# Three instead of two seven-product pairs per gate-up group of an encoder layer, with the weight sums formed by adding transfers

## The chip, the cores and the metric

The kernel runs on one core of one Trainium2 chip. Its time is the device time of one execution in microseconds (us). The engines are TensorE (PE, with its weight loads, PEld), VectorE (DVE), ScalarE (ACT), GpSimd (POOL) and SyncE (SP), which here issues transfers only.

## The reference

One layer of an encoder works on x of 256 x 2048 in float32: two gated feed-forward blocks with a mixer between them (an input projection, a bidirectional gated recurrence in eight heads, windowed attention in eight heads, an output projection). The change touches the two feed-forward blocks:

```python
D_MODEL, SEQ, D_FF = 2048, 256, 5632
def swiglu(x, w_gate_up, w_down):
    gate, up = jnp.split(x @ w_gate_up, 2, axis=-1)
    return (jax.nn.silu(gate) * up) @ w_down
ff = swiglu(rms_norm(x, pre_norm_ffn1), w_ffn1_gate_up, w_ffn1_down)
x = x + 0.5 * rms_norm(ff, post_norm_ffn1)
...                                     # the mixer
ff = swiglu(rms_norm(x, pre_norm_ffn2), w_ffn2_gate_up, w_ffn2_down)
x = x + 0.5 * rms_norm(ff, post_norm_ffn2)
```

Gate-up multiplies 256 x 2048 by 2048 x 11264, down 256 x 5632 by 5632 x 2048.

## The kernel before

**Matmuls in three products.** A float32 operand is split into two parts of a shorter format: ACT casts it to its high part (`h`), DVE subtracts that from the source to get the low part (`l`; `split_act`, lines 175 to 177). A product is then h·h + h·l + l·h, three matmuls of 128x512 outputs (`three`, line 417). All weights are split like this as they come in: SP issues the load of a pair's weights, 2 x 128 rows by 1024 columns, into a `raw` tile of 128x2048 (three of these), and each half of it, 128x1024, is cast by ACT and subtracted by DVE into `h` and `l` tiles (five each). PE reads these.

**Pairs, plain and of seven products.** A pair `u` of row blocks meets two column blocks and two halves (m) of the 256 tokens: a 2x2 by 2x2 block product. Plain, that takes eight block products, 24 matmuls. `seven` (line 445) does it as a Strassen-like scheme with seven, 21 matmuls. It needs sums of the weight blocks b11, b12, b21, b22 and of the activations' blocks. The weights' sums are made by DVE in the raw tile: line 455 writes b11+b12 and b12+b22 over the first two blocks (one instruction of 128x1024), line 459 adds to b22, line 461 to b21 (128x512 each); splits of b11, of the lower half, the upper half and the lower half again lie between. Four of the products go into PSUM banks of their own (`p`), three straight into the running sums `c`. `fold` (line 489) adds the p banks to c behind the last seven of a group.

**Gate-up** (`Gated`, line 793) goes over 11 groups `g` of 512 gate and 512 up columns, each over eight pairs of rows. In groups 1 to 10 the pairs 2 and 4 (`MIXED_IN`) are sevens; group 0 is plain in all pairs, as the sums of activations for these pairs are prepared in it (`even`, line 860, behind `spread`; the result is an `xs` tile per pair). Behind each group `units` (line 881) multiplies silu(gate) by up into `z` and `s`, and behind the first pair of the next group PE transposes them into two banks, four transposes each; ACT and DVE split the result into `ht`, the activations of down. For those pairs of down that are sevens (`MIXED`, 11 of 22), ACT first copies the bank to `z` (line 905) and DVE forms the sums of activations (`sums_of`, line 378) into a tile that stays.

**Down** (`Pairs`, line 540) goes over its 22 pairs twice, once for each half of the 2048 columns, in the order of a hand-written list per run. 11 pairs in each run are sevens. Their activations' sums are split anew in each run into an `sp` tile (`left_sums`, line 569), except for pairs 0 and 2, which the second run takes over.

**What sets the order.** Each engine runs its instructions in the order of the program; semaphores hold an instruction until its operands are there and its target is free. PSUM has eight banks, four each for the names `pa` and `pb`: four for c, four for p or transposes, handed on in turn. Loads are issued by SP as raw tiles come free.

Of the kernel before, what the change touches and what calls it, by code (L numbers as in the profile page):

```python
# [37 lines left out]
def hymba_layer_kernel(  # L38
# [347 lines left out]

    class Blocks:
# [4 lines left out]
        AHEAD = False  # L392
        ahead = None
# [43 lines left out]

        def one_block(self):

            return (  # L440
                p.tile([P, 1024], F32R, tag=t, name=nm(t))[:, 0:512]
                for p, t in ((hip, "h"), (lop, "l"))
            )

        def seven(self, u, aside=None):

            raw = load(self.source(u))
            if aside:
# [6 lines left out]
            nc.vector.tensor_tensor(  # L455
                four[:, 0:2], four[:, 0::3], four[:, 1:2].to_broadcast([P, 2, 512]), ALU.add
            )
            lower = split_half(raw, 1)
            nc.vector.tensor_tensor(b22, b11, b22, ALU.add)  # L459
            upper = split_half(raw, 0)  # L460
# [79 lines left out]
    class Pairs(Blocks):  # L540
# [7 lines left out]
        def __init__(self, w, orders, tiles, sums, room, gain_src, keep=()):  # L548

            super().__init__(tiles, sums)  # L550
            self.keep, self.kept = keep, {}
# [17 lines left out]
        def left_sums(self, u):  # L569
            if u in self.kept:  # L570
                return self.kept[u]
            keep = self.now == 0 and u in self.keep
            tag = f"sp{u}" if keep else "sp"
            w = far["pool"].tile([P, 4, 2, P], F32R, tag=tag, name=nm("sp"), bufs=1 if keep else 2)
            split_act(w[:, :, 0, :], w[:, :, 1, :], self.sums[u])
            if keep:
                self.kept[u] = w
            return w

# [11 lines left out]
        def folded(self):  # L591
            if self.now == 0:
                wide = self.room.tile([P, 2, 512], F32, tag="sp", name=nm("y"), bufs=2)
                y = [
                    [
                        self.room.tile([P, 512], F32, tag="z", name=nm("y")),
                        self.room.tile([P, 512], F32, tag="s", name=nm("y")),
                    ],
                    [wide[:, i, :] for i in range(2)],
                ]  # L600
            else:
# [185 lines left out]
    MIXED_IN = (2, 4)  # L787
# [5 lines left out]
    class Gated(Blocks):  # L793
# [11 lines left out]
        def source(self, u):  # L805
            return self.w[:, 2 * u : 2 * u + 2, :, self.g * 512 : (self.g + 1) * 512]

# [29 lines left out]
    def ffn(gated, w_dn, post_gain, again, gain=None, lead=None, aside=None):  # L837

        with ExitStack() as st:
# [5 lines left out]
            where_X_was = []  # L845

            def room_for(tag):
                return work.tile([P, 512], F32, tag=tag, name=nm(tag))

            def sums_room(u):  # L850
                n = MIXED.index(u)
                if n == 0:
# [677 lines left out]
```

## Time and profile before

Three executions took 1866.74, 1863.61 and 1865.3 us, median 1865.3. The profile was taken of a further execution, of which it gives the span, from the first instruction to the last:

| | us |
|---|---|
| median of three executions | 1865.3 |
| profiled execution: span | 1861.4 |
| what the median has beyond that span | 3.9 |
| PE busy | 1840.7 |
| DVE busy | 1576.6 |
| ACT busy | 1086.1 |
| POOL busy | 21.4 |

"Busy" is the time in which an engine has an instruction under way; a PE that is busy without a gap is not therefore at its peak. The groups name line, engine, operation, target and source tiles, shapes and count, then total and mean duration and the idle time ahead of them with what released it. A stretch is a piece of the span with the busy time of each engine in it, the granted clock of PE, the mean busy share of the 16 DMA engines and what they moved.

### The profile page before, as it was taken

How to read it: one execution, taken by the hardware profiler on the slowest of the kernel's cores; microseconds unless marked ns; L12 is line 12 of the kernel's file. 1: busy time of each engine (PE TensorE's matmuls, PEld its weight loads, DVE VectorE, ACT ScalarE, POOL GpSimd, SP SyncE). 2: the span in 40 equal slices, each digit the busy share in tenths (PEclk: the TensorE clock that was granted, in tenths of full speed). 3: DMA queues.
4: the chain of work that ended last, by engine and by line, in shares of the span. 5: the costliest groups of instructions: out<-in, count | busy, mean ns of one | idle time of the engine just before them, and what ended most of it. 6: DMA issues, size and time to landing. Idle time of an engine off the chain costs nothing.

```text
span 1861.4 us, 23279 instructions
## 1 busy us (share of the span) xinstructions
PE 1840.7 (99%) x8658; PEld 1527.0 (82%) x8658; DVE 1576.6 (85%) x1988; ACT 1086.1 (58%) x1445; POOL 21.4 (1%) x39
## 2 busy tenths in 40 slices
PE   9999999999999999999999999999999999999997
PEld 6888888888878777888888887788888888878886
DVE  7978888888899998567787788888888788899997
ACT  6555555555566565676677655655555555566563
POOL 1000000000000000000000000000000000000000
PEclk9999999999999999999999999999999999999999
DMA  7555655555555465655565455565565556445564
GB/s 251 204 200 187 208 196 181 181 203 203 188 204 215 179 255 196 201 181 166 169 187 148 169 210 200 185 214 186 211 207 192 199 195 207 175 181 205 224 228 168
DMA packets 180880, 365.78 MB, mean 197 GB/s; under 512 B 9256, under 2 KB 56448, under 8 KB 180000
## 3 DMA queue, kind: packets, MB, share of 16 engines
q1 hardware_dynamic: 180416, 364.17, 56.2%
q8 instruction: 68, 1.11, 0.2%
q14 instruction: 44, 0.36, 0.1%
q0 software_dynamic: 352, 0.14, 0.0%
HBM read 360.06 MB, written 4.21 MB: 196 GB/s over the span
## 4 chain that ended last, share of the span: by engine, by line
PE 72%; DVE 17%; DMA 4%; ACT 3%; issue 3%; POOL 0%; SPq 0%; DVEq 0%; ACTq 0%; POOLq 0%
PE pa L423 28%; PE pb L423 26%; DVE l L177 9%; PE pa L299 8%; PE pa L304 4%; DMA raw<-in_w_ffn_down_dram 2%; DVE raw L455 2%; ACT h L176 2%; DVE raw L459 1%; DVE raw L461 1%; DVE la L177 1%; DMA raw<-in_w_ffn_gate_up_dram 1%; PE pa L354 1%; PE pa L352 1%; PE pa L353 1%
## 5 line engine op out<-in xcount | busy, mean ns | idle before, releaser
L176 ACT CAST h<-raw 128x1024 fp32r<-128x1024 f32 (+1 forms) x793 | 795.0, 1028 | 616.2 <-PE pb L423 316.7
L177 DVE TENSOR_TENSOR l<-raw,h 128x1024 fp32r<-128x1024 f32 (+1 forms) x793 | 925.9, 1192 | 202.3 <-ACT h L176 168.8
L423 PE MATMUL pa<-h,xt 128*128 128x512 f32 x1248 | 431.3, 392 | 0.0
L423 PE MATMUL pb<-h,xt 128*128 128x512 f32 x1168 | 407.3, 390 | 0.0
L423 PEld LDWEIGHTS pa<-h,xt 128*128 128x128 f32 x1248 | 234.1, 188 | 48.7 <-ACT h L176 0.8
L423 PEld LDWEIGHTS pb<-h,xt 128*128 128x128 f32 x1168 | 219.2, 188 | 46.0 <-DVE xt L232 0.5
L423 PE MATMUL pa<-l,xt 128*128 128x512 f32 x624 | 243.3, 390 | 0.1
L423 PE MATMUL pb<-l,xt 128*128 128x512 f32 x584 | 227.3, 389 | 0.0
L299 PE MATMUL pa<-xt,h 128*128 128x512 f32 x672 | 164.7, 394 | 0.0
L423 PE MATMUL pa<-h,ht 128*128 128x512 f32 x440 | 156.1, 390 | 0.4 <-ACT h L176 0.4
L423 PE MATMUL pb<-h,ht 128*128 128x512 f32 x440 | 155.0, 390 | 0.2
L299 PEld LDWEIGHTS pa<-xt,h 128*128 128x128 f32 x672 | 123.0, 188 | 23.6
L423 PEld LDWEIGHTS pa<-l,xt 128*128 128x128 f32 x624 | 117.2, 188 | 24.5 <-DVE l L177 1.1
L423 PEld LDWEIGHTS pb<-l,xt 128*128 128x128 f32 x584 | 109.7, 188 | 22.6
L455 DVE TENSOR_TENSOR raw<-raw 128x1024 f32<-128x1024 f32 x88 | 107.5, 1222 | 1.6
L423 PEld LDWEIGHTS pa<-h,ht 128*128 128x128 f32 x440 | 82.4, 188 | 18.7 <-ACT h L176 1.3
L423 PEld LDWEIGHTS pb<-h,ht 128*128 128x128 f32 x440 | 82.6, 188 | 17.9 <-DVE pb L501 1.0
L304 PE MATMUL pa<-xt,l 128*128 128x256 f32 x672 | 91.5, 285 | 0.0
L304 PEld LDWEIGHTS pa<-xt,l 128*128 128x128 f32 x672 | 87.1, 191 | 3.2
L423 PE MATMUL pa<-l,ht 128*128 128x512 f32 x220 | 86.2, 392 | 1.5 <-DVE l L177 1.5
L423 PE MATMUL pb<-l,ht 128*128 128x512 f32 x220 | 86.0, 391 | 0.1
L423 PE MATMUL pb<-h,sp 128*128 128x512 f32 x192 | 70.1, 395 | 2.3 <-ACT h L176 2.3
(281 smaller groups left out, 2179.4 us busy)
## 6 DMA issues: line engine op xcount, KB each, us to landing
raw<-in_w_ffn_gate_up_dram SPq DMA_DIRECT2D x350, 512.0 KB, 4.6
raw<-in_w_ffn_down_dram SPq DMA_DIRECT2D x88, 1024.0 KB, 5.4
raw<-in_w_mix_in_dram SPq DMA_DIRECT2D x52, 1024.0 KB, 5.0
raw<-in_w_mix_out_dram SPq DMA_DIRECT2D x16, 1024.0 KB, 5.0
pg<-in_post_norm_ffn_dram SPq DMA_DIRECT2D x4, 512.0 KB, 6.9
X<-in_x_dram SPq DMA_DIRECT2D x2, 1024.0 KB, 7.4
bias<-row SPq DMA_DIRECT2D x16, 128.0 KB, 4.6
kept<-X SPq DMA_DIRECT2D x2, 1024.0 KB, 4.9
```

The lines of the kernel that those rows point to most:

```text
L176: nc.scalar.copy(hi, src)
L177: nc.vector.tensor_tensor(lo, src, hi.bitcast(F32), ALU.subtract)
L299: nc.tensor.matmul(slot[f], weights(hs, kk, f), xcol(xt, k), start=(k == 0), stop=(k == KT - 1))
L304: nc.tensor.matmul(slot[f][:, 0:T], weights(ls, kk, f), xcol(xt, kh * 8 + kk, 0), start=False, stop=False,)
L352: nc.tensor.matmul(dst, xh, h[:, o : o + n], start=(k == 0), stop=False)
L353: nc.tensor.matmul(dst, xh, l[:, o : o + n], start=False, stop=False)
L354: nc.tensor.matmul(dst, xl, h[:, o : o + n], start=False, stop=(k == KT - 1))
L423: nc.tensor.matmul(self.bank(at), lhs, rhs, start=(n == 1), stop=n in (ends, self.of[at]), skip_group_check=n > ends,)
L455: nc.vector.tensor_tensor(four[:, 0:2], four[:, 0::3], four[:, 1:2].to_broadcast([P, 2, 512]), ALU.add)
L459: nc.vector.tensor_tensor(b22, b11, b22, ALU.add)
L461: nc.vector.tensor_tensor(b21, b22, b21, ALU.add)
```

## The change

- `MIXED_IN` becomes (1, 3, 5): three sevens per group in groups 1 to 10. With pair 5 as the last seven, the fold goes to the beginning of pair 7 (before: of pair 6).
- A class `Summed` keeps two slots of 128x1024 in the room in which x was. A slot gets b11 and b12 by a transfer on POOL's queue, then b12 and b22 by an adding transfer on top, and holds then what line 455 made. When a seven has split its upper half the slot is free, and is filled for the seven after the next one of the list. SP loads only b11 and, together, b21 and b22 for such a seven.
- All 30 sevens of a gate-up do that, and in down every second one in the order of a run (6 of 11); the other sevens of down, and those of the output projection, keep the instruction on DVE.
- The sums of activations for down are split once, when they are made, in a third slot of that room, and stored to DRAM by POOL; down loads them (`left_early`, on SP, ahead of the weights of that seven). `z` and `s` live in the fourth slot.
- `units` does all eight transposes before the copies and splits.

```diff
+    class Summed:
...
+        def fill(self, slot):
+            if self.n == len(self.jobs):
+                return
+            key, (k0, n1) = self.jobs[self.n]
+            self.n += 1
+            two = slot.rearrange("p (i c) -> p i c", i=2)
+            nc.gpsimd.dma_start(two, k0)
+            nc.gpsimd.dma_start(two, n1, accum_op=ALU.add)
+            self.filled[key] = slot
+
+        def take(self, key):
+            return self.filled.get(key)
+
+        def free(self, key):
+            self.fill(self.filled.pop(key))
...
         def seven(self, u, aside=None):
 
-            raw = load(self.source(u))
+            two = self.summed.take(self.key(u)) if self.summed else None
+            self.left_early(u)
+            if two is None:
+                raw = load(self.source(u))
+            else:
+                raw = rawp.tile([P, 2048], F32, tag="raw", name=nm("raw"))
+                src = self.blocks(u)
+                nc.sync.dma_start(raw[:, 0:512], src[:, 0, 0])
+                nc.sync.dma_start(
+                    raw[:, 1024:2048].rearrange("p (i c) -> p i c", i=2), src[:, 1]
+                )
...
-            nc.vector.tensor_tensor(
-                four[:, 0:2], four[:, 0::3], four[:, 1:2].to_broadcast([P, 2, 512]), ALU.add
-            )
+            if two is None:
+                nc.vector.tensor_tensor(
+                    four[:, 0:2], four[:, 0::3], four[:, 1:2].to_broadcast([P, 2, 512]), ALU.add
+                )
+                two = raw
             lower = split_half(raw, 1)
-            nc.vector.tensor_tensor(b22, b11, b22, ALU.add)
-            upper = split_half(raw, 0)
+            nc.vector.tensor_tensor(b22, two[:, 0:512], b22, ALU.add)
+            upper = split_half(two, 0)
+            if two is not raw:
+                self.summed.free(self.key(u))
             nc.vector.tensor_tensor(b21, b22, b21, ALU.add)
...
         def left_sums(self, u):
-            if u in self.kept:
-                return self.kept[u]
...
+            if u in self.left:
+                return self.left.pop(u)
+            w = far["pool"].tile(
+                [P, 4, 2, P], F32R, tag="sp", name=nm("sp"), bufs=4 if self.stored else 2
+            )
+            if self.stored:
+                nc.sync.dma_start(w.bitcast(F32), self.sums[u])
+            else:
+                split_act(w[:, :, 0, :], w[:, :, 1, :], self.sums[u])
             return w
...
-    MIXED_IN = (2, 4)
+    MIXED_IN = (1, 3, 5)
...
-                for j in range(2):
-                    bank = (pa, pb)[j]()
+                banks = [pa(), pb()]
+                for j, bank in enumerate(banks):
                     for i in range(2):
...
+                for bank in banks:
                     g = len(hts)
...
-                        sums[g] = sums_of(u, sums_room(g))
+                        ws = sums_of(u, room_for("s").rearrange("p (j t) -> p j t", j=4))
+                        w = where_X_was(2).rearrange("p (j i t) -> p j i t", j=4, i=2)
+                        split_act(w[:, :, 0, :].bitcast(F32R), w[:, :, 1, :].bitcast(F32R), ws)
+                        sums[g] = dram.tile([P, 4, 2, P], F32, tag=f"ss{g}", name=nm("ss"))
+                        nc.gpsimd.dma_start(sums[g], w)
...
+                        if u == 6:
+                            gated.summed = Summed(
...
+            rows.summed = Summed(
+                gated.summed.slots,
+                [
+                    ((now, u), (b[:, 0], b[:, :, 1]))
+                    for now in range(2)
+                    for u in [u for u in orders[now] if u in sums][::2]
+                    for b in [rows.blocks(u, now)]
+                ],
+            )
+            rows.summed.begin()
```

Three places show what moves. First PE behind a group boundary of the first feed-forward block, from the last transpose on; `pa` and `pb` are PSUM banks, `xt` the activations, `xs` their sums. Before, the next pair is plain:

```order
L898 MATMUL pb_435_2395<-ident_79,s_422_2340 128x128
L423 MATMUL pa_423_2343<-h_438_2406,xt_11_123 128x512
L423 MATMUL pa_423_2343<-l_439_2407,xt_11_123 128x512
L423 MATMUL pa_423_2343<-h_438_2406,xt_11_123 128x512
L423 MATMUL pa_424_2344<-h_438_2406,xt_11_123 128x512
L423 MATMUL pa_424_2344<-l_439_2407,xt_11_123 128x512
L423 MATMUL pa_424_2344<-h_438_2406,xt_11_123 128x512
L423 MATMUL pb_425_2345<-h_438_2406,xt_11_123 128x512
```

The same place now:

```order
L955 MATMUL pb_558_3142<-ident_79,rooms_71_475 128x128 x4
L450 MATMUL pa_571_3188<-h_563_3168,xt_11_123 128x512
L450 MATMUL pa_571_3188<-l_564_3169,xt_11_123 128x512
L450 MATMUL pa_571_3188<-h_563_3168,xt_11_123 128x512
...
L450 MATMUL pb_574_3191<-h_567_3177,xs_72_480 128x512
L450 MATMUL pb_574_3191<-l_568_3178,xs_72_480 128x512
L450 MATMUL pb_574_3191<-h_567_3177,xs_72_480 128x512
L450 MATMUL pb_573_3190<-h_569_3184,xs_72_480 128x512
L450 MATMUL pb_573_3190<-l_570_3185,xs_72_480 128x512
L450 MATMUL pb_573_3190<-h_569_3184,xs_72_480 128x512
```

Where a plain pair went on in the c banks, a seven takes new banks at once: pa_571 first, and pb_573, the sixth of its seven block products (p2), is the bank that pb_558, the second transposes, had. The written-out order holds 7270 matmuls of 128x512, 60 fewer than before.

Second, DVE from the end of `units`' product to the splits of the transposed banks (`ht`) and the sums of activations. Before:

```order
L177 TENSOR_TENSOR l_574_3126<-raw_572_3122,h_573_3125 128x512
L455 TENSOR_TENSOR raw_572_3122<-raw_572_3122 128x1024
L177 TENSOR_TENSOR l_576_3131<-raw_572_3122,h_575_3130 128x1024
L459 TENSOR_TENSOR raw_572_3122<-raw_572_3122 128x512
L461 TENSOR_TENSOR raw_572_3122<-raw_572_3122 128x512
L177 TENSOR_TENSOR l_578_3136<-raw_572_3122,h_577_3135 128x1024
L177 TENSOR_TENSOR ht_564_3073<-z_563_3071,ht_564_3073 128x2x256
L380 TENSOR_TENSOR sums_109_681<-z_563_3071 128x256
L177 TENSOR_TENSOR ht_566_3084<-pb_565_3079,ht_566_3084 128x2x256
```

And now:

```order
L177 TENSOR_TENSOR l_566_3173<-raw_562_3165,h_565_3172 128x1024
L177 TENSOR_TENSOR l_568_3178<-rooms_71_475,h_567_3177 128x1024
L501 TENSOR_TENSOR raw_562_3165<-rooms_71_475,raw_562_3165 128x512
L505 TENSOR_TENSOR raw_562_3165<-raw_562_3165 128x512
L177 TENSOR_TENSOR l_570_3185<-raw_562_3165,h_569_3184 128x1024
L177 TENSOR_TENSOR l_577_3217<-raw_575_3213,h_576_3216 128x1024
L177 TENSOR_TENSOR ht_559_3152<-rooms_71_475,ht_559_3152 128x2x256
L380 TENSOR_TENSOR rooms_71_475<-rooms_71_475 128x256
L177 TENSOR_TENSOR ht_561_3162<-pb_558_3142,ht_561_3162 128x2x256
```

The double sum is gone (the slot in `rooms` holds it), and behind the seven's last split one split of the following pair (l_577) now stands ahead of the two `ht` splits.

Third, POOL in the first feed-forward block. Before, it has no weights to move:

```order
L186 TENSOR_TENSOR r_49_374<-v_48_372,mhalf_86 128x1
L186 TENSOR_TENSOR r_57_390<-v_56_388,mhalf_86 128x1
L1048 DMA row_539<-bias_rows_533 8x512
L186 TENSOR_TENSOR r_1128_5881<-v_1127_5879,mhalf_86 128x1
```

Now it has these (`ss` is a stored tile of sums):

```order
L186 TENSOR_TENSOR r_49_374<-v_48_372,mhalf_86 128x1
L403 DMA rooms_71_475<-in_w_ffn1_gate_up_dram 128x2x512
L186 TENSOR_TENSOR r_57_390<-v_56_388,mhalf_86 128x1
L403 DMA rooms_71_475<-in_w_ffn1_gate_up_dram 128x2x512
L404 DMA rooms_71_475<-in_w_ffn1_gate_up_dram 128x2x512 x2
L1131 DMA row_536<-bias_rows_530 8x512
L403 DMA rooms_71_475<-in_w_ffn1_gate_up_dram 128x2x512
L404 DMA rooms_71_475<-in_w_ffn1_gate_up_dram 128x2x512
L973 DMA ss_105_696<-rooms_71_475 128x1024
```

A fill (L403) and its add (L404) stand in turn, three of each to a group, and a store of sums (L973) after every third add; the add waits on POOL for its own fill to land.

More of the change, by code (lines that the diff above doesn't have):

```diff
@@ L385, in sums_of, with __init__, begin @@
         return w
+    class Summed:
+        def __init__(self, slots, jobs):
+            self.slots, self.jobs = slots, list(jobs)
+            self.filled, self.n = {}, 0
+        def begin(self):
+            for slot in self.slots:
+                self.fill(slot)
+        def fill(self, slot):
[11 more added lines that the diff above has]
+            self.fill(self.filled.pop(key))
     class Blocks:
         AHEAD = False
+        summed = None
         ahead = None
@@ L436, in plain, with left_early @@
             self.three(("c", m, n), a[:, k, 0, ms], a[:, k, 1, ms], hs[k][:, cs], ls[k][:, cs])
+        def left_early(self, u):
+            pass
         def one_block(self):
@@ L546, in hymba_layer_kernel, with __init__ @@
         AHEAD = True
-        def __init__(self, w, orders, tiles, sums, room, gain_src, keep=()):
+        def __init__(self, w, orders, tiles, sums, room, gain_src, stored=False):
             super().__init__(tiles, sums)
-            self.keep, self.kept = keep, {}
+            self.stored, self.left = stored, {}
             self.w, self.orders = w, orders
@@ L569, in left_sums, with left_early, key, blocks @@
         def left_sums(self, u):
-            if u in self.kept:
-                return self.kept[u]
[L572 to L577, printed above, removed]
-            return w
+            if u in self.left:
[7 more added lines that the diff above has]
+                split_act(w[:, :, 0, :], w[:, :, 1, :], self.sums[u])
+            return w
+        def left_early(self, u):
+            if self.stored:
+                self.left[u] = self.left_sums(u)
+        def key(self, u):
+            return self.now, u
+        def blocks(self, u, now=None):
+            now = self.now if now is None else now
+            src = self.w[u * 2 * P : (u + 1) * 2 * P, now * 1024 : (now + 1) * 1024]
+            return src.rearrange("(k p) (n c) -> p k n c", p=P, n=2)
         def one_block(self):
@@ L592, in folded @@
             if self.now == 0:
[L593 to L599, printed above, removed]
+                wide = [
+                    self.room.tile([P, 2, 512], F32, tag="sp", name=nm("y"), bufs=3)
+                    for _ in range(2)
                 ]
+                y = [[t[:, i, :] for i in range(2)] for t in wide]
             else:
```

36 lines of the change are left out of this document (23 added, 13 removed).

## The prediction

> **What bounds the kernel now.** I read the page first, then the stretches (a table of busy time by window), the groups by shape in a steady stretch of gate-up, the waits, and last the timeline of one group boundary. The page's head gives the busy time of each engine.
>
> ```profile
> span 1861.4 us, 23279 instructions
> PE 1840.7 (99%) x8658; PEld 1527.0 (82%) x8658; DVE 1576.6 (85%) x1988; ACT 1086.1 (58%) x1445; POOL 21.4 (1%) x39
> ```
>
> TensorE (PE) is busy 1840.7 of 1861.4 us, so only 20.7 us of the span could be won without taking work from it. The stretches show that this holds stage by stage. After the two ends stand the length, busy time of PE, its weight loads, DVE, ACT and POOL, the granted clock, the DMA share and GB/s. Rows one and four are starts (the first 20 us; group 0 of the first gate-up), rows two and three steady gate-up, five and six the two down products.
>
> ```profile
> 0.00:20.00 20.00, 18.21 (x75) 11.85 (x76) 11.55 (x28) 12.16 (x25) 4.93 (x14) 1.00 0.88 314
> 250.00:350.00 100.00, 100.00 (x451) 82.99 (x450) 84.21 (x97) 54.55 (x61) 0.00 (x0) 1.00 0.58 201
> 1500.00:1600.00 100.00, 100.00 (x451) 82.96 (x450) 82.17 (x94) 52.21 (x60) 0.00 (x0) 1.00 0.55 189
> 40.00:80.00 40.00, 39.55 (x178) 31.98 (x179) 38.92 (x53) 18.05 (x22) 0.55 (x1) 1.00 0.53 184
> 470.00:715.00 245.00, 241.74 (x1051) 194.50 (x1050) 233.75 (x264) 146.83 (x177) 0.00 (x0) 1.00 0.59 216
> 1628.00:1830.00 202.00, 200.18 (x870) 161.83 (x870) 197.01 (x221) 125.40 (x150) 0.00 (x0) 1.00 0.57 211
> ```
>
> In gate-up PE has no gap at all while DVE is busy 82 to 84%: there every matmul taken away is time, as long as nothing else becomes late. In down DVE is busy 95% (233.75 of 245) and 98% (197.01 of 202), and PE idles 3.26 and 1.82 us. Group 0 of the first gate-up has DVE at 97% (38.92 of 40). The clock is at 1.00 throughout and stays out of the sum.
>
> What a matmul costs in the stream comes from the timeline, since busy times of neighbours overlap. This is PE at a group boundary: start, duration, line, tiles.
>
> ```profile
> 1535.39 0.39 PE L423 MATMUL pa<-h,xt 128*128 128x512 f32 x1
> ...
> 1540.60 0.39 PE L423 MATMUL pb<-h,xt 128*128 128x512 f32 x1
> 1540.84 0.27 PE L898 MATMUL pa<-ident,z 128*128 128x128 f32 x1
> ...
> 1541.60 0.27 PE L898 MATMUL pb<-ident,s 128*128 128x128 f32 x1
> 1541.63 0.48 PE L423 MATMUL pa<-h,xt 128*128 128x512 f32 x1
> 1541.94 0.40 PE L423 MATMUL pa<-l,xt 128*128 128x512 f32 x1
> ```
>
> From 1535.39 to 1540.60 lie 23 steps: 5.21/23 = 0.2265 us for each 128x512 product. The eight transposes take until the next stream's start, some 0.87 us (0.79, and the next step, 0.31, is 0.08 longer than the others). A group of gate-up is now six plain pairs of 24 matmuls and two sevens of 21: 186 x 0.2265 + 0.87 = 43.0 us.
>
> **The change part by part.** *The third seven.* Each of the 10 groups behind group 0 gets one more pair of 21 instead of 24 matmuls, in both FFNs: 20 x 3 = 60 fewer, and the written-out order of PE does hold 60 fewer. 60 x 0.2265 = -13.6 us, all in stretches where PE has no gap. Down keeps its sevens, so PE gains nothing there. A group becomes 183 x 0.2265 + 0.87 = 42.3 us.
>
> *VectorE.* The groups by shape of 150 to 450 us (count, busy us, mean ns, idle before), and the page's row of the sum that goes:
>
> ```profile
> L177 DVE TENSOR_TENSOR l<-raw,h 128x1024 fp32r<-128x1024 f32 x126 | 150.8, 1222 | 49.2 <-ACT h L176 48.5
> L459 DVE TENSOR_TENSOR raw<-raw 128x512 f32<-128x512 f32 x14 | 9.6, 688 | 0.2
> L461 DVE TENSOR_TENSOR raw<-raw 128x512 f32<-128x512 f32 x14 | 9.7, 692 | 0.5
> L177 DVE TENSOR_TENSOR l<-raw,h 128x512 fp32r<-128x512 f32 x14 | 9.6, 683 | 0.0
> L455 DVE TENSOR_TENSOR raw<-raw 128x1024 f32<-128x1024 f32 x88 | 107.5, 1222 | 1.6
> L177 DVE TENSOR_TENSOR sp<-sums,sp 128x512 fp32r<-128x512 f32 x28 | 19.2, 684 | 0.0
> L177 DVE TENSOR_TENSOR sp<-su,sp 128x512 fp32r<-128x512 f32 x12 | 8.2, 685 | 0.0
> ```
>
> A plain pair costs DVE two splits, 2.44 us. A seven costs 3 x 1.222 + 0.683 + 0.688 + 0.692 + 1.222 (the double sum L455) = 6.95 us now, and 5.73 us when the transfer adds. A group's weights: six plain and two sevens, 28.6 us, become five and three, 29.4 us; the split of the sums for down that moves here adds 0.685. So DVE has 1.5 us more per group in a time that is 0.7 us shorter: 82-84% becomes about 88%. On average that is hidden beside PE; where it pinches is below. Were DVE the bound, it would have to pass 42.3 us, and it lacks some 5.
>
> In down DVE loses 12 double sums per FFN (14.7 us) and 20 splits of sums (13.7 us; 40 of the two rows above over two FFNs, none left), 28 us of the 200 to 234 in each window: 95 to 98% becomes some 84%. The PE gaps there, 5.1 us in the two windows, are what can come back: I take -3 (0 to -5.1), as transfers hold ACT there too, which these rows of the waits show (who, on what: us, times, mean).
>
> ```profile
> ACT h L176 <- DMA raw<-in_w_ffn_down_dram: 19.8, 13, 2.9
> ACT h L176 <- DMA raw<-in_w_ffn_gate_up_dram: 24.5, 32, 3.9
> ```
>
> *Group 0* stays plain, but prepares the sums of activations for a third pair, between its own splits. By these rows (count, busy, mean ns):
>
> ```profile
> L869 DVE TENSOR_TENSOR z<-xt 128x512 f32<-128x512 f32 x4 | 2.7, 684 | 0.0
> L380 DVE TENSOR_TENSOR s<-z 128x256 f32<-128x256 f32 x4 | 1.7, 419 | 0.0
> L383 DVE TENSOR_TENSOR s<-s,z 128x128 f32<-128x128 f32 x4 | 1.1, 281 | 0.0
> L384 DVE TENSOR_TENSOR s<-z,s 128x128 f32<-128x128 f32 x4 | 1.1, 280 | 0.0
> L177 DVE TENSOR_TENSOR xs<-s,xs 128x512 fp32r<-128x512 f32 x4 | 2.7, 686 | 0.5 <-ACT xs L176 0.5
> ```
>
> 0.68 + 0.42 + 0.28 + 0.28 + 0.69 = 2.35 us for each FFN. DVE is at 97% in the first FFN's group 0, so it counts there, less in the second: +2.4 of a possible +4.7.
>
> *The bank hand-over at a group boundary.* Today 24 plain products follow the transposes. Now pair 1, a seven, follows at once, and its product p2 takes the second transposes' bank, the sixth group of three: PE gets there 0.87 + 15 x 0.2265 = 4.27 us after the first transpose. DVE frees that bank with its split of ht from pb:
>
> ```profile
> 1539.44 1.22 DVE L177 TENSOR_TENSOR l<-raw,h 128x1024 fp32r<-128x1024 f32 x1 [1.08 <-ACT h L176]
> 1540.70 0.69 DVE L459 TENSOR_TENSOR raw<-raw 128x512 f32<-128x512 f32 x1
> 1541.42 0.69 DVE L461 TENSOR_TENSOR raw<-raw 128x512 f32<-128x512 f32 x1
> 1542.16 1.23 DVE L177 TENSOR_TENSOR l<-raw,h 128x1024 fp32r<-128x1024 f32 x1
> 1543.30 0.69 DVE L177 TENSOR_TENSOR ht<-z,ht 128x512 fp32r<-128x512 f32 x1
> 1543.91 0.42 DVE L380 TENSOR_TENSOR su<-z 128x256 f32<-128x256 f32 x1
> 1544.24 0.68 DVE L177 TENSOR_TENSOR ht<-pb,ht 128x512 fp32r<-128x512 f32 x1
> ```
>
> The split now ends at 1544.92, 4.08 us after the first transpose at 1540.84: 0.19 us to spare, in a place where it isn't needed so early. In the new order one more 128x1024 split of the next pair stands ahead of it. If that comes in full, the stall is 1.22 - 0.19 = 1.0 us in each of 20 groups, +21; if it falls into DVE's idle time (1.08 us ahead of the first row), nothing. I take 0.2 x 20 = +4, near the lower end, since that split needs a cast by ACT which comes no earlier for a late DVE and the idle time is nearly as long as the split.
>
> *The fold* moves from the start of pair 6 to that of pair 7, in order to stand two pairs behind pair 5 as it stood behind pair 4; no instruction more. Taken as 0; its cover is the 128x512 split that stands in its way now instead of a 128x1024 one (0.683 for 1.222).
>
> *The transfers.* These are the rows of the page on landing (KB each, us from issue to landing):
>
> ```profile
> raw<-in_w_ffn_gate_up_dram SPq DMA_DIRECT2D x350, 512.0 KB, 4.6
> raw<-in_w_ffn_down_dram SPq DMA_DIRECT2D x88, 1024.0 KB, 5.4
> ```
>
> A gate-up pair is two of them, 1.05 MB; eight in 43.0 us are 195 GB/s, as the windows say. A seven now moves 0.79 MB on SP and 2 x 0.52 on POOL's queue, and each group stores 0.52 of sums: 5 x 1.05 + 3 x 1.84 + 0.52 = 11.3 MB in 42.3 us, 266 GB/s. Down: 16 x 1.05 + 6 x 1.84 + 11 x 0.52 = 33.6 MB in 495 x 0.2265 = 112 us, 300 GB/s. By the windows 189 GB/s are a share of 0.55 and 314 of 0.88, so a full share is an estimated 345 to 357 GB/s: the transfers fit, at 0.76 and 0.85.
>
> The place that they must reach in time: a slot is free behind the upper split of pair 1 and its next content is read by pair 5's second sum. PE is 21 + 24 + 21 + 24 = 90 matmuls, 20.4 us, further on then; less that sum and the split behind it (0.69 + 1.22) leaves 18.5 us. POOL fills, waits, and adds. No row shows a transfer of this size from POOL, nor an adding one. POOL's rows, with DVE's beside the last:
>
> ```profile
> 5.21 0.52 POOL L115 DMA_DIRECT2D rows<-rn_lower_bounds_fwd_dram  x1
> 23.99 0.54 POOL L1042 DMA_DIRECT2D bias_rows<-in_onehot_dram  x1 [16.30 <-DMA raw<-in_w_ffn_gate_up_dram]
> 19.75 5.32 DVE L177 TENSOR_TENSOR l<-raw,h 128x1024 fp32r<-128x1024 f32 x4 [0.19 <-ACT h L176]
> ```
>
> An issue of 8 rows took 0.52, one of 32 rows and 64 KB 0.54; 256 rows lie between 0.7 (by rows) and 4.3 us (by bytes, eight times 0.54). With landings of 4.6 to 5.4 a fill and an add take 2 x (0.7 + 5.0) = 11.4 us, at worst 2 x (4.3 + 5.4) = 19.4. I take the first, as the two rows hardly grow with size: 7 us to spare, cost 0, lower bound 0 since nothing gets shorter. Behind POOL's waiting add queue the other slot's fill and the store of sums, which have a group's time, and one inverse root of the FFN's start behind the first fill: 0 to +1, taken 0.
>
> *A page against a row.* The Trainium skill's "SBUF — State Buffer", section "Who interferes with whom", says that a POOL-issued DMA can look stalled by VectorE because GpSimd lacks port time to write descriptors, though not for tensor_tensor, the only form that splits use; the trace agrees so far, 0.54 us amid the four splits from 19.75 and 0.52 elsewhere. By a full block of one 1.2 us split per issue the 11.4 would be 13.8, still in time.
>
> **The sum.** -13.6 + 4 (hand-over) + 2.4 (group 0) - 3 (down) = -10.2 against the profiled 1861.4: a span of 1851.2. The median of the runs, 1865.3, is 3.9 above that span, so the time is 1855.1 us.
>
> **The rivals.** *Late transfers (slower).* An adding transfer has to read its target too; if that counts, gate-up moves 266 + 37 = 303 GB/s and down 300 + 28 = 328, of some 350. The landings grow with the load, 4.6 to about 7 us, and the place where that decides is the refill for pair 5 (18.5 us) or the raw load of the next group's pair 0. That load gets its room after pair 5's last split; before DVE comes to its first half stand four splits and two adds of the fold, 4 x 1.22 + 2 x 0.69 = 6.3 us, less ACT's cast about 5.2. What comes later than that and outlasts the h and l tiles costs 20 us per us over 20 groups; 0.7 late undoes the gain, 1.5 late is +30: 1861.4 - 10.2 + 30 + 3.9 = 1885. For it speaks the unshown rate; against it that 0.88 was reached at 314 GB/s and that the h and l tiles hold more than two pairs ahead. The Trainium skill's "Collectives: The Full Stack", section "The bandwidth ceiling: the fold count and why AG ≠ RS ≠ AR", says that a reduce in the DMA engines runs at half of a copy since it has two source reads; no row here shows an add, and by it the fill and add would be an estimated 0.7 + 5 + 0.7 + 10 = 16.4 us, just in time. Chance 0.22.
>
> *The hand-over eats the gain.* A stall of 0.7 us a group instead of 0.2 is +10: 1865, no change; it decides from 0.2 upwards and DVE at 88% speaks for it. Chance 0.15.
>
> *All of it hidden.* No hand-over stall and down's whole 5.1: 1861.4 - 13.6 + 2.4 - 5.1 + 3.9 = 1849. Chance 0.10.
>
> *The change doesn't do what it says.* Excluded: the 60 matmuls are gone from the order and 24 of down's 44 double sums with them.
>
> **How the numbers follow.** The forecast (hand-over at 0 to 0.4 us, down at -1 to -5) spans 1850 to 1859 and has 0.48; 0.05 is for what I haven't seen. A measurement can tell about 0.2%, 3.7 us, here. Faster: 0.48 + 0.10 + 0.03 of the hand-over case + 0.01 = 0.62; same 0.14; slower 0.22 + 0.02 = 0.24. The range reaches from 1846 (all hidden, group 0 free) to 1873, where the late transfers cost 18 us; some 0.17 lies outside, mostly above.
>
> **What would show it.** Right: 8598 or so PE records, 60 fewer; gate-up windows with PE without a gap and DVE near 88% at 260 to 300 GB/s; group boundaries 42.3 us apart; PE waits on DVE's ht split of at most 0.4 us a group; down windows with DVE near 84% and smaller PE gaps; POOL's adds landing within 15 us of the slot's release. Wrong: waits of the second sum or of ACT on the POOL transfers or on raw loads that PE shows as gaps, a share near 1, POOL issues of several us, or group boundaries 43 us and more apart.

## The result and the profile after

The change makes the kernel slower: four executions took 1904.2 to 1926.4 us, median 1911.4, beside 1864.5 of the kernel before. The ratio is 1.026 (95% interval 1.022 to 1.030), 47 us where a gain of 10 was forecast. The profiled execution is the longest of the four, so its parts sum to 63 us more than the profiled one of before; medians are compared where a price is named.

The head of the page, the queues and the landings (KB each, median us) of the changed kernel:

```profile
span 1924.6 us, 23724 instructions
PE 1856.9 (96%) x8598; PEld 1521.9 (79%) x8598; DVE 1556.2 (81%) x1996; ACT 1105.3 (57%) x1469; POOL 193.2 (10%) x229
...
q1 hardware_dynamic: 179456, 365.22, 55.6%
q0 software_dynamic: 38464, 99.76, 21.5%
...
raw<-in_w_ffn_gate_up_dram SPq DMA_DIRECT2D x290, 512.0 KB, 6.7
raw<-in_w_ffn_down_dram SPq DMA_DIRECT2D x64, 1024.0 KB, 6.8
rooms<-in_w_ffn_gate_up_dram POOLq DMA_DIRECT2D x120, 512.0 KB, 6.6
...
sp<-ss SPq DMA_DIRECT2D x44, 512.0 KB, 7.9
```

The 60 matmuls are gone (8598 records) and DVE has less to do, 81 for 85%, yet PE is idle more: 96 for 99%. The loads of weights that landed in 4.6 and 5.4 us now take 6.7 and 6.8. The two queue rows point to the adds. POOL's queue moves 99.76 MB in 21.5% of the engines' time, SP's 365.22 MB in 55.6%: 0.216 and 0.152 points per MB, 1.42 times as much. Of POOL's bytes 84 x 0.524 = 44.0 MB are adds; if its fills and stores cost what SP's loads cost, the adds cost 1 + 0.42 x 99.76 / 44.0 = 1.9 times that. The packet records say the same: an adding packet of 2 KB takes 178 ns at the median, a plain one of 2 KB on SP's queue 84.

From one boundary of groups to the next PE takes 43.0 to 47.9 us, where it took 43.05 in 18 of the 20 groups before (42.7 and 43.1 in the other two). This is one of them (246 to 292 us, 46.3 us long) in stretches of 10 us, with the steady gate-up as a whole ahead (the columns are those of the prediction's windows):

```profile
150.00:450.00 300.00, 291.36 (x1279) 236.43 (x1278) 243.30 (x294) 166.94 (x194) 43.58 (x48) 0.99 0.83 248
...
250.00:260.00 10.00, 10.00 (x45) 8.09 (x44) 8.82 (x13) 6.44 (x8) 1.95 (x3) 1.00 1.02 319
260.00:270.00 10.00, 10.00 (x46) 8.29 (x45) 7.85 (x9) 5.62 (x7) 1.96 (x2) 1.00 0.95 264
270.00:280.00 10.00, 9.13 (x41) 7.17 (x39) 7.39 (x9) 4.83 (x6) 1.21 (x1) 1.00 1.06 328
...
285.00:295.00 10.00, 10.00 (x50) 8.35 (x49) 6.67 (x8) 6.10 (x8) 0.74 (x1) 1.00 0.26 86
```

The second last column is what to read. Over 300 us the DMA engines are busy 0.83, which looks like room to spare; inside the group they are full for 30 us, and then at 0.26 around the boundary. All refills fall behind pairs 1, 3 and 5. DVE is not the bound in any of these rows. (A packet counts in the stretch in which it starts, so a share can pass 1.)

What that does to PE is seen at the end of the full stretch. The load of the second half of pair 7's weights was issued at 261.70 us and landed at 273.70, 12.0 us later; in the run with all sums on DVE, below, no raw load of the group from 237 to 280 us took over 6 us. ACT (first) waits for the second half of pair 7's weights, DVE behind it:

```profile
273.80 1.05 ACT L176 CAST h<-raw 128x1024 fp32r<-128x1024 f32 x1 [2.28 <-DMA raw<-in_w_ffn_gate_up_dram]
275.16 1.06 ACT L176 CAST h<-raw 128x1024 fp32r<-128x1024 f32 x1 [0.32 <-DMA raw<-in_w_ffn_gate_up_dram]
```

```profile
271.55 1.23 DVE L177 TENSOR_TENSOR l<-raw,h 128x1024 fp32r<-128x1024 f32 x1 [0.47 <-ACT h L176]
274.88 1.23 DVE L177 TENSOR_TENSOR l<-raw,h 128x1024 fp32r<-128x1024 f32 x1 [2.10 <-ACT h L176]
276.02 0.68 DVE L540 TENSOR_TENSOR rooms<-pb,rooms 128x512 f32<-128x512 f32 x1
...
280.27 0.69 DVE L544 TENSOR_TENSOR pa<-pa,rooms 128x512 f32<-128x512 f32 x1
```

The fold (L540 to L547) stands behind pair 7's splits in DVE's queue. So a raw load for which ACT waits 2.3 us delays the fold although the fold needs nothing of it, and PE, which has done the six products of the first bank, waits for L544, the sum into the second:

```profile
278.74 0.39 PE L450 MATMUL pa<-h,xt 128*128 128x512 f32 x1
281.02 0.50 PE L450 MATMUL pa<-h,xt 128*128 128x512 f32 x1 [1.89 <-DVE pa L544]
...
282.43 0.63 PE L450 MATMUL pa<-l,xt 128*128 128x512 f32 x1
282.85 0.63 PE L450 MATMUL pa<-h,xt 128*128 128x512 f32 x1
283.28 0.63 PE L450 MATMUL pb<-h,xt 128*128 128x512 f32 x1
```

```profile
280.00:285.00 5.00, 3.98 (x11) 3.11 (x12) 4.55 (x7) 0.69 (x1) 0.00 (x0) 0.66 0.72 236
```

Behind the wait of 1.89 us the products come 0.42 us apart, not 0.23: the window shows a granted clock of 0.66 on average, by the trace's record of the clock 0.5 for 3.41 us and 1 for the rest. That costs 3.41 / 2 = 1.7 us, nearly as much as the wait. The 20 groups of this run take 904.8 us, 53 more than 20 of 42.57 us, which is what a group takes without a stall (below). PE's waits in them sum to 32.9 us, and six stretches at half clock cost 10.2; the rest, some 0.5 us a group, is not accounted for here. Over the whole run the waits read (who, on whom: us, times, longest):

```profile
ACT h L176 <- DMA raw<-in_w_ffn_down_dram: 69.6, 31, 5.9
ACT h L176 <- DMA raw<-in_w_ffn_gate_up_dram: 65.2, 56, 4.9
PE pa L450 <- DVE pa L544: 26.4, 17, 2.0
```

ACT waited for these loads 19.8 and 24.5 us before. The adds on POOL's queue wait too, this is their group:

```profile
L404 POOL DMA_DIRECT2D rooms<-in_w_ffn_gate_up_dram x60 | 72.4, 1207 | 318.4 <-DMA rooms<-in_w_ffn_gate_up_dram 313.6
```

An add takes POOL 1.2 us to issue and waits 5.3 us for its fill; that costs POOL's time alone, as no engine waits for a filled slot in the list of waits.

### The profile page after: what moved, and what is told of

Read it like the earlier page. It is cut to its first block, busy times and chain, and to the rows that moved or that the text cites. A ratio compares the mean times of both kernels' runs of the same rounds, so it can differ in the third digit from the quotient of the medians.

```text
span 1924.6 us, 23724 instructions
## 1 busy us (share of the span) xinstructions
PE 1856.9 (96%) x8598; PEld 1521.9 (79%) x8598; DVE 1556.2 (81%) x1996; ACT 1105.3 (57%) x1469; POOL 193.2 (10%) x229
## 3 DMA queue, kind: packets, MB, share of 16 engines
q1 hardware_dynamic: 179456, 365.22, 55.6%
q0 software_dynamic: 38464, 99.76, 21.5%
## 4 chain that ended last, share of the span: by engine, by line
PE 47%; DVE 21%; DMA 17%; ACT 7%; issue 6%; SPq 0%; POOL 0%; ACTq 0%; DVEq 0%; POOLq 0%
PE pa L450 15%; PE pb L450 15%; DVE l L177 11%; DMA raw<-in_w_ffn_gate_up_dram 11%; PE pa L299 8%; DMA raw<-in_w_ffn_down_dram 6%; ACT h L176 6%; PE pa L304 4%; DVE raw L501 2%; DVE raw L505 2%; PE pa L352 1%; PE pa L354 1%; PE pa L353 1%; DVE rooms L543 1%; DVE pa L544 1%
## 5 line engine op out<-in xcount | busy, mean ns | idle before, releaser
L177 DVE TENSOR_TENSOR l<-raw,h 128x1024 fp32r<-128x1024 f32 (+1 forms) x749 | 863.1, 1177 | 239.8 <-ACT h L176 208.0
L176 ACT CAST h<-raw 128x1024 fp32r<-128x1024 f32 (+1 forms) x749 | 739.2, 1015 | 532.2 <-DVE raw L505 217.5
L450 PE MATMUL pa<-h,xt 128*128 128x512 f32 x1168 | 413.6, 398 | 29.5 <-DVE pa L544 26.4
L450 PE MATMUL pb<-h,xt 128*128 128x512 f32 x1048 | 372.0, 397 | 2.9 <-DVE pb L545 2.0
L450 PEld LDWEIGHTS pb<-h,xt 128*128 128x128 f32 x1048 | 200.0, 191 | 51.2 <-DVE pb L547 4.8
L450 PE MATMUL pb<-l,xt 128*128 128x512 f32 x524 | 206.1, 393 | 0.0
L404 POOL DMA_DIRECT2D rooms<-in_w_ffn_gate_up_dram x60 | 72.4, 1207 | 318.4 <-DMA rooms<-in_w_ffn_gate_up_dram 313.6
L177 DVE TENSOR_TENSOR l<-rooms,h 128x1024 fp32r<-128x1024 f32 x84 | 102.4, 1219 | 0.8 <-ACT h L176 0.8
L176 ACT CAST h<-rooms 128x1024 fp32r<-128x1024 f32 x84 | 88.2, 1050 | 8.1 <-PE pb L450 7.5
L450 PE MATMUL pb<-h,xs 128*128 128x512 f32 x240 | 86.6, 397 | 0.4 <-DVE ht L177 0.4
```

Of the source, the lines that this page charges most:

```text
L176: nc.scalar.copy(hi, src)
L177: nc.vector.tensor_tensor(lo, src, hi.bitcast(F32), ALU.subtract)
L404: nc.gpsimd.dma_start(two, n1, accum_op=ALU.add)
L450: nc.tensor.matmul(self.bank(at), lhs, rhs, start=(n == 1), stop=n in (ends, self.of[at]), skip_group_check=n > ends,)
```

## The experiments

Theory A: adding transfers take the DMA engines double time, the engines are full for most of a group, the last raw loads of the group land late, and the fold and PE behind them. Theory B: the third seven with its later fold and its bank hand-over is too tight by itself. Theory C: GpSimd's serial queue. All medians below stand beside the kernel before on the same chip, 1864 to 1866 us.

**The same transfers without adding.**

```diff
-            nc.gpsimd.dma_start(two, n1, accum_op=ALU.add)
+            nc.gpsimd.dma_start(two, n1)
```

> The second transfer of each pair of fills overwrites instead of adding (the sums of weights are then wrong; bytes, queue, waits and order stay). Theory A, the adds fill the DMA engines in the stretch of pairs 1 to 5 (their 2 KB packets take 178 ns at the median, plain ones 84 ns) and the raw load of pair 7, behind whose split the fold stands, comes late: the loads land in about 5.5 us instead of 6.7, groups take 42.5 to 43.7 us instead of 43.5 to 47.9, time 1858 to 1880. Theory B, the third seven with its later fold and its bank hand-over is itself too tight: groups stay at 45 us on average, time 1900 or more. Theory C, GpSimd's serial issuing (each add waits there for its fill) is the limit: time falls only a little, 1890 to 1905.

Measured: 1880.7 us, ratio 1.008 (1.007 to 1.010), 31 us less than the change. The page of this run:

```profile
span 1877.3 us, 23724 instructions
...
q0 software_dynamic: 27712, 99.76, 15.3%
...
raw<-in_w_ffn_gate_up_dram SPq DMA_DIRECT2D x290, 512.0 KB, 5.9
```

Same bytes on POOL's queue, but 15.3% of 1877.3 = 287 us of all engines instead of 21.5% of 1924.6 = 414. The 127 us belong to 84 adds: 1.5 us each, on top of the 287 / 190 = 1.5 us that one of its 190 transfers takes (84 fills, 84 copies, 22 stores). An add costs twice a copy. The copies go in packets of 4 KB, 159 ns at the median, where the adds go in packets of 2 KB; as two plain packets of 2 KB take 168 ns, the size of the packets isn't what doubles the time.

```profile
150.00:450.00 300.00, 298.98 (x1338) 244.92 (x1337) 255.99 (x309) 174.34 (x203) 34.28 (x49) 1.00 0.77 264
```

With copies the share is 0.77, close to the 0.76 of the forecast, and PE loses 1 of 300 us. 14 of the 20 groups are 42.5 to 43.3 us long here. Theory A gave 1858 to 1880 and is missed by 0.7 us only; B gave 1900 or more and C 1890 to 1905, and both fall as the main cause.

**No adds at all, sums by DVE.** `summed` stays `None` in both products, line 496 forms every double sum.

> Three sevens per group as in the change, but every double sum is made by VectorE, nothing is filled or added by transfers; stored sums of activations stay. Theory A: DVE has 39.4 + 3 x 1.22 = 43.1 us per group, so the groups take 43.1 to 44 us, down is near the kernel before or a little better: 1862 to 1880, with loads landing in about 4.7 us. Theory B: the fold and the bank hand-over stall as in the change, and a busier DVE makes it worse: 1905 or more.

1864.7 us, ratio 1.000 (0.999 to 1.001). 15 of the 20 groups take 42.55 to 42.60 us, below the 43.1 to 44 that theory A gave:

```profile
1300.00:1600.00 300.00, 300.00 (x1348) 247.37 (x1347) 282.50 (x328) 174.08 (x203) 3.19 (x6) 1.00 0.61 211
```

DVE is busy 282.5 of 300 us and PE has no gap. I had counted 43.1 us of DVE work for a group, which was too much, as neighbours on DVE overlap by some 0.08 us each (a split of 1.22 us is followed after 1.14). So theory B falls: with everything on DVE the third seven fits. And the reason for moving sums off DVE is gone too: at 94% it held up nothing in these groups.

**Two sevens with adds.** `MIXED_IN = (2, 4)`, all else as in the change.

> Sevens on pairs 2 and 4 as before, with fills and adds in gate-up and down as in the change. Theory A: the adds are a third fewer in gate-up, so the share of 1.0 lasts shorter; groups 43.1 to 44.5 us, down as slow as in the change (about +8 a product): 1870 to 1895. Theory B: with the third seven the gate-up loss goes altogether: groups 43.05 us, 1858 to 1866.

1889.5 us, 1.013 (1.011 to 1.014): slower without any third seven, where B gave 1858 to 1866. Of the 24 us, ten lie in the groups of both blocks and 13 in the two downs. But eleven of the 20 groups are back at 43.05 us, and this run has a third fewer adds in gate-up as well as no third seven, so by itself it doesn't tell the two apart; the runs with one to three adds do.

**The fold ahead of pair 7's casts and splits.**

```diff
+                    elif self.pos == self.after + 1:
+                        raw = load(self.source(u))
+                        self.fold()
+                        hs, ls = split(raw)
...
-                    if self.pos == self.after + 1:
+                    if self.pos == self.after + 1 and False:
```

> The change with the fold issued behind the load of pair 7 but ahead of its two casts and splits, so that a late load of pair 7 no longer holds the fold. Theory A: TensorE's wait on the fold, 0.4 to 2.9 us in most groups and followed by 3.4 us at half clock, goes in most groups; what is left of the late load is met by the h and l tiles or by TensorE at pair 7 itself: 1875 to 1895. If the fold is late for another reason (ACT's copy, VectorE's queue), the time stays within 1900 to 1925.

1903.0 us, 1.020 (1.018 to 1.021), 8 us less than the change; that is outside the 1875 to 1895 of theory A and within the range that was given for a fold that is late for another reason. DVE's timeline shows that the edit hardly did what it was for:

```profile
357.87 0.68 DVE L540 TENSOR_TENSOR rooms<-pb,rooms 128x512 f32<-128x512 f32 x1
360.34 1.22 DVE L177 TENSOR_TENSOR l<-raw,h 128x1024 fp32r<-128x1024 f32 x1 [1.79 <-ACT h L176]
361.48 0.69 DVE L541 TENSOR_TENSOR pa<-pa,rooms 128x512 f32<-128x512 f32 x1
```

A split that waits for a late load now stands between the fold's first and second step, as the order of DVE is the scheduler's. In 14 of the 20 groups it waits 0.9 to 2.2 us there. So the place was not tested by this run; the timelines above remain the evidence for it.

**Adds in gate-up alone** (`rows.summed = None`).

> The change with down's double sums all on VectorE; gate-up keeps its fills and adds. Theory A (the DMA engines' time that the adds take): each down then takes as long as with all sums on VectorE, 234.3 instead of 242.7 us from its first to its last product, and the gate-up groups stay at 43.5 to 48 us: 1890 to 1900. Rival: down is slow because of the stored sums that it loads, not because of the adds: it stays at 240 us and more, 1903 to 1912.

1898.3 us, 1.017 (1.014 to 1.020). The first down takes 234.6 us, as with all sums on DVE (234.3), and 242.7 in the change. The stored sums that it still loads are not what made it slow.

**Three rooms for the sums of activations.** From here on all double sums are DVE's, and the question is what else is in the way. At the start of down ACT waits for POOL's store of pair 20's sums before it can cast pair 21's (run with all sums on DVE):

```profile
508.81 0.62 ACT L176 CAST rooms<-rooms 128x512 fp32r<-128x512 f32 x1 [2.59 <-DMA ss<-rooms]
509.33 2.94 ACT L176 CAST h<-raw 128x1024 fp32r<-128x1024 f32 x3
```

```diff
-                        w = where_X_was(2).rearrange("p (j i t) -> p j i t", j=4, i=2)
+                        w = where_X_was(len(sums) % 3).rearrange("p (j i t) -> p j i t", j=4, i=2)
```

> All double sums on VectorE, three sevens, and three rooms in turn for the split sums of activations in place of one. Theory: at the start of down ACT waits 2.6 us for the store of pair 20's sums to leave the one room before it can cast pair 21's, and casts of weights stand behind it, so that TensorE stalls 2.05 and 2.55 us there; both stalls go: 1858 to 1862. Rival: VectorE is late there anyhow (it makes both pairs' sums beside the weights): the stalls stay over 1.5 us and the time within 1863 to 1866.

1865.4 us, 1.000 (1.000 to 1.001), and the stalls stayed at 2.5 and 2.7 us. The edit missed: `sums` is filled up ahead of these two pairs, so both got the same room. It is mended below.

**Pair 1's sums of activations made in group 1.**

```diff
-                if u in MIXED_IN:
+                if u in MIXED_IN[1:]:
+                    summed_in(u)
...
+                    if g == 1 and u == 5:
+                        summed_in(1)
```

> As with three rooms, and the sums of activations for the pair 1 sevens are made in group 1, behind its pair 5, instead of in group 0; group 1 has two sevens. Theory: the third pair's sums overload VectorE in group 0 (transposes wait 2.6 us for the product in the second block, the first group takes 44.9 instead of 42.6 us in the first); 3 matmuls more per block (+1.4 us) buy off 2 to 3 us per block: 1855 to 1860. Rival: the waits come from the switch of ACT's table and the raw loads there, and stay: 1860 to 1864.

1856.0 us, 0.995 (0.994 to 0.997): 9.4 us less than the run before it, although six matmuls (1.4 us) were added. PE's wait of 2.6 us for the product behind the second block's group 0 is gone, and the first group of the first block takes 43.3 instead of 44.9 us.

**Stored sums loaded behind the weights of their seven.** `left_early` moves below `load`.

> As the one with the later sums, and each load of stored sums is issued behind the weights of its seven instead of ahead of them. Theory: in down the 512 KB ahead of the weights delay them (landing 6.1 instead of 5.4 us) and their casts; behind them they are needed only by the third product: down 1 to 2 us shorter each, 1852 to 1858. Rival: the engines share their time among all transfers under way, the order does nothing: as the one with the later sums, within 1.5 us.

1856.0 us, 0.995 (0.994 to 0.997): the order of the two loads does nothing.

**Rooms by the pair's place.** `where_X_was(MIXED.index(g) % 3)`.

> As the one with the later sums, with the rooms taken by the pair's place among the sevens of down, so that pairs 20 and 21 have different rooms (in the runs before they had the same one, as the list that the index came from was full by then). Theory: ACT's wait of 2.6 to 3.0 us for the store of pair 20 goes, and with it the stall of TensorE of 2.5 to 2.7 us at the start of each down and the 3.4 us at half clock behind it (1.7 us lost): up to 8 us less, 1847 to 1852. Rival: VectorE or the loads are late there anyhow: stalls over 1.5 us stay, 1854 to 1857.

1849.6 us, 0.992 (0.990 to 0.993). The stalls at the start of down went, with the half clock behind them: 6.4 us for two waits of 2.6 us.

**One, two and three adds per group.** To this kernel the fills and adds of gate-up are given back for pair 3; for pairs 1 and 5; and for all three (group 1 has two sevens, so 20, 38 and 58 adds). Down has none. As the slots take one or two of the rooms, the stored sums share the others; pairs 20 and 21 keep different ones. The run with two:

```diff
-                        w = where_X_was(MIXED.index(g) % 3).rearrange("p (j i t) -> p j i t", j=4, i=2)
+                        w = where_X_was(1 if g == 21 else 2).rearrange("p (j i t) -> p j i t", j=4, i=2)
...
-                                    for u in MIXED_IN
+                                    for u in (1, 5)
+                                    if (g, u) != (1, 1)
...
-                            gated.summed = None
+                            gated.summed.begin()
```

> As the one with the rooms by place, and pair 3 of each group from 1 on takes its double sum from a fill and an add (a third of the adds of the change, one slot, none in down). Theory A (adds cost the DMA engines double, and hurt only where the engines are full): about 0.7 of a share on average, no share of 1.0 for longer than a few us; groups stay within 0.1 us of 42.57 us: within 3 us of the run without adds, and no gain, since VectorE at 94% is not late anywhere in a group. Rival 1, any add on POOL's queue harms: a third of the loss that gate-up's adds showed (33 us), +8 to +12. Rival 2, VectorE's 1.2 us less per group shows: -3 or better.

> As the run with one add per group, but pairs 1 and 5 of each group (pair 5 alone in group 1) take their double sums from fills and adds, 38 adds instead of 20, in two slots; no add in down. Theory A (harm only where the engines are full): the share of a whole group rises from about 0.67 to about 0.73, still with room; most groups within 0.5 us of 42.57 us, 1848 to 1858. Rival, harm in proportion to the adds (33 us for 60 in gate-up): +21 against none, about 1870.

> The run with two adds per group, with fills and adds for all three sevens of a group (58 adds in all, pairs 3 and 5 alone in group 1), none in down. Theory A, a threshold: the stretch from pair 1 to pair 5 stands at a share of about 1.0, raw loads land in over 6 us, the fold comes late in most groups with half clock behind it: 20 to 40 us more than with two adds, 1870 to 1890. Rival: the late groups of the change came from its stalls in group 0 and at the start of down, which put the transfers out of step: without these three adds cost as little as two, 1850 to 1858.

Measured: 1848.2 (0.992, 0.990 to 0.993), 1851.7 (0.992, 0.991 to 0.994) and 1883.6 us (1.011, 1.009 to 1.012). The same stretch of the runs with none, one, two and three, each from its own profile:

```profile
150.00:450.00 300.00, 300.00 (x1348) 247.26 (x1347) 283.20 (x332) 175.96 (x207) 3.72 (x7) 1.00 0.61 209
```

```profile
150.00:450.00 300.00, 300.00 (x1347) 247.16 (x1346) 272.86 (x325) 175.91 (x207) 17.56 (x21) 1.00 0.71 227
```

```profile
150.00:450.00 300.00, 299.77 (x1349) 246.81 (x1347) 265.15 (x316) 175.72 (x205) 30.93 (x35) 1.00 0.79 246
```

```profile
150.00:450.00 300.00, 292.08 (x1288) 237.66 (x1288) 243.53 (x292) 169.58 (x197) 44.77 (x49) 0.99 0.85 256
```

DVE falls step by step from 283 to 265 us and PE gains nothing by it; the DMA share climbs from 0.61 to 0.79 and PE loses nothing by that either. With the third add, at 0.85, PE loses 8 of 300 us. So in these runs it is a threshold, not a price per add, and it is there without the stalls at the start of down and without the third pair's work in group 0. The landings of raw loads go with it, 4.8, 5.0, 5.0 and 6.5 us. In stretches of 10 us the run with two adds has shares of 0.96, 0.77, 0.97 and 0.50 (239 to 279 us); the one with three has 0.95, 1.04, 0.93 and 0.37 (250 to 290 us), and PE loses 1.8 us in the third of them. Whether the third add harms by its number or by its place between the other two was not tested.

**Two sevens, sums of activations stored, no adds.** `MIXED_IN = (2, 4)`, rooms by place.

> Sevens on pairs 2 and 4 as before, all double sums on VectorE, sums of activations for down stored and loaded, rooms by place. This leaves only the stored sums of the change. Theory: gate-up groups at 43.05 us, 60 - 6 = 54 matmuls more than the run with the later sums (12.2 us): 1859 to 1865, so the stored sums bring next to nothing and the third seven is what brings the gain. Rival: the stored sums bring the gain (VectorE's 28 us in down less): 1850 to 1856.

1861.0 us, 0.998 (0.997 to 0.999): the stored sums by themselves bring 3.8 us, and the third seven the rest.

**Adds in down alone**, on the kernel with pair 1's sums later (1856.0 us).

> The run with the later sums (1856.0 us) with adds for every second seven of down as in the change and none in gate-up. Theory A: 6 adds per run beside 11 loads of stored sums bring down's share from about 0.72 to about 0.9, each down takes 4 to 8 us longer: 1864 to 1872. Rival: in down the adds cost nothing by themselves, the loss there came from gate-up's late transfers: 1854 to 1858.

1869.6 us, 1.003 (1.002 to 1.004): 13.5 us more. Down's stretch in this run, and in the kernel without these adds:

```profile
500.00:720.00 220.00, 212.62 (x912) 172.31 (x911) 183.55 (x200) 118.86 (x137) 17.05 (x20) 0.98 0.89 291
```

```profile
500.00:720.00 220.00, 215.94 (x941) 176.11 (x941) 200.60 (x218) 122.39 (x146) 1.26 (x3) 0.99 0.72 265
```

DVE is relieved by 17 us, PE loses 3.3. From their first to their last product the two downs take 240.9 and 238.6 us where they took 235.5 and 234.1, together 9.9 us more. Another 4.6 us lie in the steady groups of gate-up, most of them 42.8 to 43.0 us long here, although no add runs in them; why stays open. (The two kernels also differ in the rooms that gate-up's sums of activations go through, one here and three in turn there, which made no difference to the groups above.) The change beside its form with adds in gate-up alone gives a like price for down's adds, 1911.4 - 1898.3 = 13.1 us.

## Why the prediction was wrong

Term by term, in us:

| term of the sum | forecast | measured | from |
|---|---|---|---|
| 60 matmuls less, with the hand-over | -13.6 + 4 | -9.6 | 20 x (42.57 - 43.05), groups with no stall |
| group 0 | +2.4 | +10.7 | 9.4 + 1.4 for six matmuls, the run with later sums |
| down without double sums and splits | -3 | -3.8 | the run with two sevens and stored sums |
| one room for the sums, start of down | not seen | +6.4 | rooms by place |
| transfers, gate-up | 0 | +34.0 | three adds against none, 1883.6 - 1849.6 |
| transfers, down | 0 | +13.5 | adds in down alone, 1869.56 - 1856.01; 9.9 of it in the downs |

They sum to +51 where 47 were measured; the parts were taken in different kernels, and the rest isn't settled.

**Right.** The matmuls' price, the hand-over and the direction of every step off the DMA queues. In groups without a stall PE's steps from the transposes to the seven's p2 bank are together some 0.2 us longer than its rate, close to the 0.2 that was taken. The stored sums brought what was said, but without the double sums being off DVE, so the 12 adds per block in down bought nothing of it.

**Wrong, and deciding: "the transfers fit, at 0.76 and 0.85".** Two things failed in this step. The sum counted an add at the price of a copy, and an add takes 3.0 us of all engines where a copy takes 1.5: with copies the share was 0.77 and gate-up lost little. The late-transfer rival had the adds' double reading, and its 303 GB/s of some 350 came true as a share of 0.83 to 0.85; but the sum and the rival alike held a group's mean against the engines' full rate. A group has some 30 us at a share of 1 and 10 us at a quarter; what counts is whether a load that is issued in the full stretch is needed within it. I had seen that shares are means over unlike stretches for PE and DVE, and not done the same for the DMA engines.

**Wrong place.** I looked at the refill for pair 5 and at the next group's pair 0. A fill and its add took longer than the 11.4 us of the sum, 15.1 and 15.7 us in the group shown (256.19 to 271.33 and 265.36 to 281.08 us), but stayed within the 18.5, and the profile shows no engine but POOL waiting for a slot. It was pair 7's own load, and the fold behind its split. "Taken as 0; its cover is the 128x512 split" was argued from the splits' durations and left out what a split waits for. With the fold moved to pair 7, its load stands at the end of the full stretch.

**Wrong price.** A late load was to cost its lateness. In six of the 20 groups PE's wait is followed by 3.41 us at half clock, another 1.7 us. The rival's +30 for gate-up came near the measured 34.0, though at the wrong place; its 1885 was short of 1911 mainly by down's 13.5, by 8.3 of group 0 and by the 6.4 at the start of down.

**Group 0** was priced by the durations alone, 2.4 us. What the added work did was to delay the product behind which the transposes wait, and then the whole first group.

The Trainium skill's "Collectives: The Full Stack", section "The bandwidth ceiling: the fold count and why AG ≠ RS ≠ AR", gives an add in the DMA engines two reads for one write and half the rate, there for a ring of cores. Here 178 against 84 ns per 2 KB packet and 3.0 against 1.5 us per 512 KB agree with it; I had it as a rival, and the row-based sum without it was the worse one. The Trainium skill's "SBUF — State Buffer", section "Who interferes with whom", has tensor_tensor not block descriptor writing, by inference; POOL's adds took 1.2 us to issue beside a busy DVE, and nothing in these runs speaks against it.

## What to carry to other kernels

Moving work from an engine at 85 to 94% to the DMA engines pays only if that engine was late somewhere: look for a wait on it before relieving it. Judge a DMA budget by the share in stretches of a few us across the period of the loop, not by its mean, and count an adding transfer twice. And look at what is queued behind a split that waits for a load: here the harm came through instructions that needed nothing of it.

The best kernels of these runs are the third seven with all double sums on DVE, pair 1's sums in group 1 and rooms by place (1849.6 us, 0.992), and the same with one add per group (1848.2), which can't be told from it.

## What the runs showed of the hardware that was not expected

- An adding transfer into SBUF takes the DMA engines 2.1 times as long per packet as a plain one (178 against 84 ns for 2 KB), and the whole transfer twice (3.0 against 1.5 us of all 16 engines for 512 KB).
- A wait of PE of only 1.9 us can be followed by 3.41 us at half clock. Of eleven waits of 1.85 to 1.95 us in the groups of the changed kernel six were, the one of 1.89 us at 281 us among them; one of 1.95 us at 327 us in the next group was not (46.3 and 45.1 us long). The starts of the half-clock stretches tell the two kinds apart. They lie whole multiples of 3.413 us from one another, like the marks of a clock that runs on its own: from 100.68 to 148.47, to 281.59 and to 373.75 us it is 14, 39 and 27 times that. In the six cases the whole wait lies between two marks of this grid; in the other five a mark falls into it, which leaves 1.53 us at most on either side. Over all sixteen traces PE was idle for 1.89 us or more between two marks, at full clock, 39 times, and half clock followed each time; it never followed an idle time under 1.57 us, and in between it followed 5 times out of 21. The Trainium skill's "TensorE: Matmul & The Clock Gate", Part 1, names a free-running window of about 3.4 us; the length and the grid agree, but the page asks for a whole idle window, and here a shorter gap was enough.
- The DMA share of a stretch reaches 1.02 to 1.06 at 319 to 328 GB/s with adds in it.
